# Low parts of weight pages: a negative copy on ScalarE and an accumulating DMA in place of a VectorE subtraction

## The chip, the cores and the metric

One core of one Trainium2 chip. The time is that of one launch of the whole program, in microseconds (us) on the device; lower is better. The runs of the kernel before took 3516.85, 3520.6 and 3525.22 us, median 3520.6.

## What is computed

Two blocks on 1024 tokens of 1024 features, batch 1, all in float32. Cut to what matters here:

```python
# first block, two layers
for l in range(2):
    mod = silu(c) @ w_ada[l] + b_ada[l]                    # shift, scale, gate, twice
    h = rms_norm(x) * (1 + scale_a) + shift_a
    proj = h @ w_in[l]                                      # GLA (4 heads) and MLA (4 heads)
    x = x + gate_a * (concat(gla(proj), mla(proj)) @ w_out[l])
    h = rms_norm(x) * (1 + scale_f) + shift_f
    x = x + gate_f * (square(relu(h @ w_mlp_up[l])) @ w_mlp_down[l])   # 1024 -> 4096 -> 1024
# second block, one layer
z = rms_norm(x) @ w_in                                      # gMLP, RG-LRU and S5 side by side
x = x + mix(z) @ w_out
x = x + moe(rms_norm(x))                                    # 16 experts, two for each token
```

The matmuls are made to float32 accuracy. TensorE takes operands of the type fp32r, so each matrix is held as two: hi, the rounded value, and lo, the rest. A product is three matmuls, hi x hi, hi x lo (lo of the activations) and lo x hi (lo of the weights).

## The kernel before

**Weight pages.** Weights are streamed. A raw page (tag wr, two buffers; in the MLP's up product also e) comes by a load on SP's queue. `split` (L129) makes the two parts: ScalarE copies the raw page to hi (tag wh, L131), and VectorE subtracts, lo = raw - hi (tag wl, L132). There are two buffers of wh and two of wl. A raw page is free for the next load when the subtraction has read it.

```python
    def split(self, src, hi, lo, eng=None):
        self.nc.scalar.activation(hi, src, AF.Copy)
        self.split_ins = (eng or self.nc.vector).tensor_sub(lo, src, hi)
```

Three places make weight pages: `wpage` (L134; `wcols`, L143, calls it), `page` in `mlp` (L1051), and the page of the first quarters in `mlp` (L1090). Activations are split by `split` too (L1229, and the pieces in `put`, L1160 to L1168, and elsewhere), as are the weights of the experts.

**Where pages are used.** The output projection of each layer (L975 to L984) goes through eight pages of 1024 x 128 (512 KB) for the first half of the tokens and the same eight for the second; for each page it loads a piece xo of the residual on POOL's queue (L980), makes 24 matmuls into one PSUM tile (tag ps) and adds the residual on VectorE (L983). `norm_T` makes the operands B11 ... T4 of the MLP in quarters, with sums and differences of quarters.

**The MLP by seven products.** Each pair of 128-column blocks of w_mlp_up, cut into the quarters a11, a12 (upper rows) and a21, a22, goes through `seven` (L1101): POOL (GpSimd) makes s1 = a21 + a22 (L1106), s2 = s1 - a11 (L1107), a21 = a11 - a21 in place (L1108) and s4 = a12 - s2 (L1109). `page` then splits two quarters of 128 x 512 (256 KB) at a time into one wh and one wl buffer, and each quarter is multiplied with one operand by 12 matmuls (hi, hi, lo for each of the four slices). There are 16 pairs in a layer. For the first seven the first quarter's product has been made ahead, so that six products are left ("six-product pairs"); the other nine have all seven. Results get a ReLU on ScalarE, a square on ScalarE or POOL (L1083) and go to DRAM by SP's queue.

The down product runs plain groups of four rows (pages of 512 KB, `plain`, L1206), then *windows*: up to four pairs of hidden features at once, by `seven` again, over four column blocks ("units", 26 in both layers, 14 of them with four pairs), then plain groups again. Within a window `operands` (L1170) makes sums and differences of activations on POOL or VectorE, and `into_x` (L1190) adds results into x, partly on POOL (L1197). In both layers the modulation columns of a later part (w_ada times the condition) are computed beside the MLP ("ada columns"), on VectorE.

**What sets the order.** The program is written as a sequence; a scheduler places each instruction on its engine's list by its own simulated timeline before the program is compiled, with each tile's buffers given out in the order of the code. Each engine then runs its list in order and waits for semaphores. A DMA that POOL issues stands in POOL's list and waits there for its inputs, ahead of what comes after it. SP issues the weight loads, POOL and ACT some others.

Of the kernel before, what the change touches and what calls it, by code (L numbers as in the profile page):

```python
# [15 lines left out]
D = 1024  # L16
# [12 lines left out]
GD = 1  # L29
# [30 lines left out]
class Base:  # L60
    def __init__(self, nc, tc, ctx, I):
# [8 lines left out]
        self.R = ("X", "Y", "Z", "M")   # pages of x, of h's two halves, and of the phase's own  # L70
        self.uid = 0
        self.tab, self.tab_ins = None, []   # the ACT table load in force, and what has used it
# [25 lines left out]
    # ---- small helpers  # L98
# [3 lines left out]
    def mm3(self, out, terms):  # L102
        """terms: list of (wh, wl, xh, xl); out = sum w^T x to float32 accuracy"""
        n = len(terms)
        for i, (wh, wl, xh, xl) in enumerate(terms):
            self.mm(out, wh, xh, start=(i == 0), stop=False)
            self.mm(out, wh, xl, start=False, stop=False)
            self.mm(out, wl, xh, start=False, stop=(i == n - 1))

    def table(self, name):  # L110
        """the ACT table set of what follows, loaded after the last use of the one before"""
        with ExitStack() as st:
            for i in self.tab_ins:
                st.enter_context(self.tc.issue_after(i))
            self.tab = self.nc.scalar.preload_act_table_set(name).ins
        self.tab_ins = []

    def act(self, *a, **k):
        """an activation that needs the table set in force"""
# [9 lines left out]
    def split(self, src, hi, lo, eng=None):  # L129
        """hi + lo == src, both float32r"""  # L130
        self.nc.scalar.activation(hi, src, AF.Copy)  # L131
        self.split_ins = (eng or self.nc.vector).tensor_sub(lo, src, hi)  # L132

    def wpage(self, pieces, a, b, eng=None, tag="wr"):  # L134
        """pieces: list of (index function on the [128,a,b] tile, dram ap)."""
# [4 lines left out]
        self.split(raw, hi, lo)  # L140
        return hi, lo

    def wcols(self, w, c0, n=128):  # L143
        """w dram [K, M]: columns c0..c0+n as [128, K/128, n]"""
# [3 lines left out]
    def rinv(self, psum, n, out, u=None):  # L148
        """out = (psum/n + eps)^-1/2; with a spare tile u, with a Newton step"""
# [21 lines left out]
    def sigmoid_(self, out, x):  # L171
        """out = sigmoid(x) for x >= -40, x in SBUF or PSUM (exp/ln table)"""
# [5 lines left out]
class Block1(Base):  # L178
# [14 lines left out]
    def cols(self):  # L193
        """per-feature vectors on partitions"""
# [17 lines left out]
    # ---- conditioning  # L212
# [7 lines left out]
    def ada_steps(self, l, js, tags=("wr",), kn=2):  # L220
        """mod columns of the vectors js of layer l, onto their biases, kn * 128 rows a step"""
# [27 lines left out]
    # ---- start  # L249
    def start(self):  # L250
        """the first half of x, and the first columns (K half 0, then 1) of the first layer's shift and scale"""
# [25 lines left out]
    def low_load(self, l, kh, i, tag):  # L277
        """columns of m_kpe and g_a with the first of m_q, or the rest of m_q with m_kv: rows of a K half"""
# [5 lines left out]
    def ada_first(self, q):  # L284
        """shift and scale of layer 0: columns of a K half"""
# [20 lines left out]
    def x_done(self, kt, hf, spill, eng=None, tag="t2"):  # L306
        """a tile of x is final: its part of the sum of squares, and its copy in DRAM"""
# [15 lines left out]
    def norm_half(self, hf, s1, sh, kts=range(NT)):  # L323
        """h of a half: rms norm of x times s1 plus sh, as hi and lo"""
# [28 lines left out]
    def adaptive(self, l, j):  # L353
        """scale and shift columns of a norm: vectors j (shift) and j + 1 (scale)"""
# [44 lines left out]
    # ---- hybrid mixer  # L399
    def weave(self, *streams):  # L400
        """streams of (generator, steps a turn), to the end of all"""
# [8 lines left out]
    def mixer(self, l, side=None):  # L410
# [12 lines left out]
        # k_pe and the gate's low rank columns, then m_q, m_kv; the first half of the tokens first  # L423
# [24 lines left out]
        # GLA q and k  # L448
# [23 lines left out]
        def norms(hf):  # L472
            """low rank norms -> hi/lo"""
# [15 lines left out]
        def decays(hf):  # L489
            """GLA gate: cumulative log decay within chunks of 128"""  # L490
# [21 lines left out]
        def pe_units():  # L512
            """rotary parts before their norms: k_pe (on both 64-partition halves) and q_pe of all heads"""
# [35 lines left out]
        def low_first():  # L549
            """the first half of the tokens, as the columns of shift and scale come"""  # L550
# [39 lines left out]
        # ---- GLA values, token-major  # L590
# [23 lines left out]
        # ---- GLA  # L614
# [4 lines left out]
        def gla_in(hf, T):  # L619
            """attention within chunks (keys on partitions), one power of two of the distance at a time"""  # L620
# [5 lines left out]
            # q with the other head's rows at zero  # L626
# [39 lines left out]
        def gla_out(hf, T):  # L666
            """outputs and state, two chunks at a time"""
# [19 lines left out]
            # q decayed from the chunk's start, with the other head's rows at zero  # L687
# [45 lines left out]
        def go_units():  # L733
            """g_o: silu, to DRAM"""
# [14 lines left out]
        # ---- MLA, beside the GLA  # L749
        scale = float(192 ** -0.5)  # L750
        mh, ml = [None] * 8, [None] * 8      # 0..3 GLA, 4..7 MLA
# [17 lines left out]
        def behind(g):  # L769
            """not before the chunks' steps of GD steps ago"""  # L770
# [17 lines left out]
        def mla_steps():  # L788
            # values of all heads, token-major
# [20 lines left out]
            def rope_stack(head):  # L810
                """hi and lo of a head's rotary part, one above the other"""
# [42 lines left out]
            def scores(head, qb):  # L854
                """scores of 128 queries, and their maximum"""
# [23 lines left out]
            def exps(banks, st):  # L879
                """probabilities times their sum, and the sum by banks"""  # L880
# [89 lines left out]
        # ---- output projection and residual, the first half of the tokens first  # L970
# [16 lines left out]
    # ---- MLP  # L987
    def norm_T(self, hf, s1, sh):
        """h of a half, as operands of the products by quarters (K halves by token halves; Strassen's, Winograd's form):
        T1 = B12 - B11, T2 = B22 - T1, T3 = B22 - B12, T4 = B21 - T2"""  # L990
# [47 lines left out]
    def mlp(self, l, following, side=None, early=None, late=()):  # L1038
# [12 lines left out]
        def page(srcs):  # L1051
            n = srcs[0].shape[1]
            hi, lo = self.pg("wh", (128, 2, n, 128), F32R), self.pg("wl", (128, 2, n, 128), F32R)
            for i, s in enumerate(srcs):
                self.split(s, hi[:, i], lo[:, i])
# [11 lines left out]
        def plus(p, t, tag=None):  # L1067
            """p + t, in t or in a tile of its own"""
# [19 lines left out]
        for u in range(NPRE + 1):  # L1088
            if u < NPRE:
# [3 lines left out]
                self.split(raw, hi, lo)  # L1093
# [6 lines left out]
        def seven(K, js, fin, m1=None):  # L1100
            """the four quarters of a product from seven products; with m1, the first quarter is there already"""  # L1101
# [51 lines left out]
        # down: tiles plainly, then windows of four pairs by quarters from the pair J0 to J, then plainly  # L1153
# [108 lines left out]
class Block2(Block1):  # L1262
# [19 lines left out]
    # ---- S5 parameters (depend on weights alone)  # L1282
    def s5_prep(self):
# [15 lines left out]
        def exp_tanh(dst, src, scale, tmp, tmp2):  # L1299
            """dst = exp(2 * scale * src)"""  # L1300
# [11 lines left out]
        # powers of the modulus, n = 0..8  # L1312
# [5 lines left out]
        # phase  # L1318
# [15 lines left out]
        def cmul_steps(dr, di, ar, ai, br, bi, tmp, eng):  # L1334
            """d = a * b (complex), d distinct from a, b"""
# [26 lines left out]
        # (lam_bar - 1) / lam  # L1362
# [14 lines left out]
        # B bar and C^T  # L1377
# [8 lines left out]
        # x -> state, as [(8 tokens, last first; 16 channels), state]  # L1386
# [9 lines left out]
        for th in range(2):  # L1396
# [13 lines left out]
            # state -> y  # L1410
# [17 lines left out]
        # response within 8 tokens, zero padded to the left  # L1428
# [20 lines left out]
        # phases of the states at the starts of 8-token chunks  # L1449
# [26 lines left out]
    # ---- S5 over 128 chunks of 8 tokens  # L1476
    def s5_x(self, w):
        """x by position in the chunk: [128 chunks, group, position (last first), channel]"""
# [24 lines left out]
    def s5(self, xt, th):  # L1503
        """outputs before the gelu: [128 chunks, position, tile, group of the tile, channel]"""
# [41 lines left out]
        # states before each chunk  # L1546
# [27 lines left out]
    def s5_gelu(self, ytm):  # L1574
        """gelu, then channels on partitions"""
# [35 lines left out]
    # ---- RG-LRU parameters  # L1611
    def lru_prep(self):
        """decay rate -8 softplus(-lambda), per channel"""
# [8 lines left out]
        # log1p(exp(-|lam|)) = 2 atanh(z), z = s / (2 - s)  # L1622
# [14 lines left out]
    def mixer2_load(self):  # L1637
        """block diagonal gates; W_s^T, with the later half of keys cut for the earlier half of positions; b_s over the rows of a head"""
# [14 lines left out]
    def lru_gates(self, bx, gt):  # L1653
        """bx becomes the gated input; also the recurrence gates and tanh(log a)"""
# [29 lines left out]
    def lru_scan(self, bx, rt):  # L1684
        """states, in place of tanh(log a)"""
        nc = self.nc
        V, G, ACT = nc.vector, nc.gpsimd, nc.scalar
        for j, (rp, thp) in enumerate(rt):
            prev = 0.0
            for hf in range(2):  # L1690
# [5 lines left out]
                # 1 - a^2 = -tanh(log a) (1 + a^2)  # L1696
# [17 lines left out]
    def sgu(self, vt, hf):  # L1714
        """v becomes W_s v + b_s"""
# [44 lines left out]
    def mixer2(self):  # L1760
# [61 lines left out]
        # ---- output projection, residual  # L1822
# [738 lines left out]
```

## Time and profile before

| | |
|---|---|
| runs | 3516.85, 3520.6, 3525.22 us; median 3520.6 |
| span of the profiled execution | 3517.2 us |
| TensorE matmul (PE) busy | 3190.6 us, 91% |
| VectorE (DVE) busy | 2557.0 us, 73% |
| ScalarE (ACT) busy | 1670.0 us, 47% |
| GpSimd (POOL) busy | 1385.6 us, 39% |
| the two subtraction groups of L132, 331 + 174 instructions | 367.1 + 178.3 us of DVE |

The profile is of one execution, and its span is the time from the first to the last instruction. An engine's busy time counts its own work; issuing a DMA is not counted. Matmuls whose weight load is hidden appear back to back, so PE at 100% in a stretch means that nothing kept it waiting there. A line number with an operation names a group of instructions; "out<-in" are the program's tiles.

### The profile page before, as it was taken

The numbers are of one execution on the slowest core, as the hardware profiler recorded it, in microseconds if no ns is written. First come the engines' busy times: TensorE is split into PE (matmuls) and PEld (weight loads), VectorE is DVE, ScalarE is ACT, GpSimd is POOL, SyncE is SP. The second block draws the span as 40 slices with busy tenths as digits, with TensorE's granted clock in tenths as the row PEclk, the third lists the DMA queues.
The fourth block names the chain that finished last, engine by engine and source line by source line (L and its number), as shares of the span: only waits on it lengthen the run. The fifth ranks groups of instructions, "written<-read, shape, count | busy, mean of one in ns | idle before, by whom it ended". The sixth has DMA issues, their size and how long they took to land. (4 is left out here: it accounts for less than half of the span.)

```text
span 3517.2 us, 42552 instructions
## 1 busy us (share of the span) xinstructions
PE 3190.6 (91%) x14714; PEld 2524.4 (72%) x14714; DVE 2557.0 (73%) x3737; ACT 1670.0 (47%) x2819; POOL 1385.6 (39%) x1176
## 2 busy tenths in 40 slices
PE   5998899899898889999898999997889999699995
PEld 3776678687776677777686788775667766588884
DVE  8778765768879998677756655779985344677867
ACT  4545764532233445556755434323445243466753
POOL 4145411663436763246303654445742313211114
PEclk9999999999999999999999999999999999899998
DMA  6433124346632224121123433522251223589974
GB/s 218 117 96 105 58 64 134 111 150 215 207 129 88 83 91 137 55 67 70 35 77 101 147 116 110 176 78 89 91 162 48 66 75 102 210 279 326 334 269 174
DMA packets 327341, 462.57 MB, mean 132 GB/s; under 512 B 25697, under 2 KB 189825, under 8 KB 327121
## 3 DMA queue, kind: packets, MB, share of 16 engines
q1 hardware_dynamic: 300496, 375.74, 33.2%
q0 software_dynamic: 25472, 83.46, 6.9%
q8 instruction: 117, 1.92, 0.2%
q14 instruction: 104, 0.84, 0.1%
q10 hardware_dynamic: 1152, 0.61, 0.1%
HBM read 383.45 MB, written 77.33 MB: 131 GB/s over the span
## 5 line engine op out<-in xcount | busy, mean ns | idle before, releaser
L131 ACT ACTIVATE wh<-wr 128x1024 fp32r<-128x1024 f32 (+5 forms) x331 | 263.1, 795 | 495.3 <-PE ps L100 314.6
L100 PE MATMUL ps<-Y,wh 128*128 128x512 f32 (+1 forms) x1454 | 475.9, 408 | 17.7 <-ACT wh L131 7.4
L132 DVE TENSOR_TENSOR wl<-wr,wh 128x1024 fp32r<-128x1024 f32 (+5 forms) x331 | 367.1, 1110 | 132.1 <-ACT wh L131 130.3
L100 PE MATMUL ps<-M,wh 128*128 128x512 f32 (+1 forms) x1174 | 382.4, 406 | 9.4 <-ACT wh L131 5.5
L100 PEld LDWEIGHTS ps<-Y,wh 128*128 128x128 f32 (+1 forms) x1454 | 278.4, 194 | 92.0 <-ACT wh L131 11.9
L100 PE MATMUL ps<-Y,wl 128*128 128x512 f32 (+1 forms) x727 | 292.2, 403 | 24.0 <-DVE wl L132 24.0
L100 PE MATMUL ps<-Z,wh 128*128 128x512 f32 (+1 forms) x882 | 281.1, 400 | 3.9 <-ACT Z L342 3.4
L2283 DVE TENSOR_TENSOR X<-Y,X 128x1024 fp32r<-128x1024 f32 x192 | 233.4, 1233 | 58.0 <-ACT X L2279 50.4
L100 PEld LDWEIGHTS ps<-M,wh 128*128 128x128 f32 (+1 forms) x1174 | 223.7, 193 | 66.6 <-ACT wh L131 8.4
L100 PE MATMUL ps<-M,wl 128*128 128x512 f32 (+1 forms) x587 | 237.8, 406 | 20.2 <-DVE wl L132 20.0
L2279 ACT ACTIVATE X<-Y 128x1024 fp32r<-128x1024 f32 x192 | 203.1, 1061 | 96.6 <-PE ps L100 46.9
L100 PEld LDWEIGHTS ps<-Z,wh 128*128 128x128 f32 (+1 forms) x882 | 165.4, 190 | 50.3 <-issue 7.9
L100 PE MATMUL ps<-X,wh 128*128 128x512 f32 (+1 forms) x562 | 181.3, 402 | 2.5 <-ACT wh L131 1.7
L132 DVE TENSOR_TENSOR wl<-a,wh 128x512 fp32r<-128x512 f32 (+3 forms) x174 | 178.3, 1031 | 7.1 <-ACT wh L131 6.6
L100 PEld LDWEIGHTS ps<-Y,wl 128*128 128x128 f32 (+1 forms) x727 | 139.4, 192 | 61.2 <-DVE wl L132 30.7
L100 PE MATMUL ps<-Z,wl 128*128 128x512 f32 (+1 forms) x441 | 174.5, 398 | 5.1 <-DVE wl L132 5.1
L100 PE MATMUL pS<-X,Z 128*128 128x512 f32 x576 | 155.8, 398 | 2.1 <-ACT Z L131 2.1
L100 PE MATMUL ps<-X,Z 128*128 128x512 f32 x576 | 154.4, 395 | 0.8 <-DVE X L2283 0.8
L100 PEld LDWEIGHTS ps<-M,wl 128*128 128x128 f32 (+1 forms) x587 | 112.7, 192 | 54.2 <-DVE wl L132 30.0
L100 PE MATMUL pS<-Y,wh 128*128 128x512 f32 x434 | 140.4, 404 | 5.3 <-ACT wh L131 3.2
L100 PE MATMUL ps<-X,tg 128*128 128x512 f32 x576 | 142.7, 395 | 1.1 <-DVE tg L132 0.6
L1106 POOL TENSOR_TENSOR a<-wr,wr 128x512 f32<-128x512 f32 (+3 forms) x38 | 46.7, 1230 | 229.8 <-DMA wr<-w_mlp_down 84.8
(856 smaller groups left out, 8109.4 us busy)
## 6 DMA issues: line engine op xcount, KB each, us to landing
Y<-expert_w_gate SPq DMA_DIRECT2D x64, 512.0 KB, 6.4
Y<-expert_w_up SPq DMA_DIRECT2D x64, 512.0 KB, 6.4
Y<-expert_w_down SPq DMA_DIRECT2D x64, 512.0 KB, 7.5
wr<-w_mlp_up SPq DMA_DIRECT2D x58, 512.0 KB, 4.1
wr<-w_mlp_down SPq DMA_DIRECT2D x58, 512.0 KB, 3.8
wr<-w_in SPq DMA_DIRECT2D x49, 512.0 KB, 3.8
bt<-w_ada SPq DMA_DIRECT2D x96, 256.0 KB, 3.4
hd<-t SPq DMA_DIRECT2D x70, 256.0 KB, 2.4
```

The costliest lines, as they stand in the source:

```text
L100: self.last_mm = self.nc.tensor.matmul(out, lhsT, rhs, start=start, stop=stop)
L131: self.nc.scalar.activation(hi, src, AF.Copy)
L132: self.split_ins = (eng or self.nc.vector).tensor_sub(lo, src, hi)
L1106: G.tensor_add(s1, a21, a22)
L2279: nc.scalar.activation(hi, raw, AF.Copy)
L2283: (nc.gpsimd if pool else nc.vector).tensor_sub(lo, raw, hi)
```

## The change

A new function `split_w` takes the place of `split` at the three places where weight pages are made outside the experts. Hi is the same copy. ScalarE then writes the negative of the raw page, rounded to fp32r, into the low part's buffer, and a DMA, issued by POOL, adds the raw page to that buffer in SBUF (accum_op add): lo = -hi + raw. VectorE has no part in it. Activations and the experts keep `split`. The rest of the diff takes out comments, which moves the line numbers after it by 7 (L1106 becomes L1113; the new copy is L138, the DMA L139).

```diff
+    def split_w(self, src, hi, lo):
+        nc = self.nc
+        nc.scalar.activation(hi, src, AF.Copy)
+        nc.scalar.activation(lo, src, AF.Copy, scale=-1.0)
+        nc.gpsimd.dma_start(lo, src, accum_op=OP.add)
...
     def wpage(self, pieces, a, b, eng=None, tag="wr"):
...
         hi, lo = self.pg("wh", (128, a, b), F32R), self.pg("wl", (128, a, b), F32R)
-        self.split(raw, hi, lo)
+        self.split_w(raw, hi, lo)
         return hi, lo
...
             for i, s in enumerate(srcs):
-                self.split(s, hi[:, i], lo[:, i])
+                self.split_w(s, hi[:, i], lo[:, i])
...
                 self.last_w = nc.sync.dma_start(raw, wu[:, 256 * u:256 * u + 128].rearrange("(k p) c -> p k c", p=128))
                 hi, lo = self.pg("wh", (128, 8, 128), F32R), self.pg("wl", (128, 8, 128), F32R)
-                self.split(raw, hi, lo)
+                self.split_w(raw, hi, lo)
```

There are 539 such splits: 156 of 128x1024 elements (512 KB), 296 of 128x512 (256 KB), 28 each of 128x128, 128x256 and 128x384, and three of 128x640, together 171 MB. The scheduler makes its lists anew, so other instructions move too.

POOL in the up product, a six-product pair, as its list was before: here s1, s2, the difference in place and s4 of a pair, then the squares of earlier results.

```order
L1106 TENSOR_TENSOR a_1155_5629<-wr_5625,e_5627 128x512
L1107 TENSOR_TENSOR a_1156_5630<-a_1155_5629,wr_5625 128x512
L1108 TENSOR_TENSOR wr_5625<-wr_5625 128x4x128
L1109 TENSOR_TENSOR a_1157_5631<-e_5627,a_1156_5630 128x512
L1083 TENSOR_TENSOR rl_5582<-rl_5582 128x512
L1083 TENSOR_TENSOR t_1142_5545<-t_1142_5545 128x512
L1083 TENSOR_TENSOR t_1147_5579<-t_1147_5579 128x512
```

The four additions stood together. The same place, POOL's list after; wl_6007 is a page of the pair before, wl_6042 is the pair's own page of s2 and s1, wl_6078 that of a21 and s4.

```order
L1113 TENSOR_TENSOR a_1214_6034<-wr_6028,e_6030 128x512
L1114 TENSOR_TENSOR a_1215_6035<-a_1214_6034,wr_6028 128x512
L139 DMA wl_6007<-wr_5913 128x4x128
L1115 TENSOR_TENSOR wr_6028<-wr_6028 128x4x128
L1116 TENSOR_TENSOR a_1216_6036<-e_6030,a_1215_6035 128x512
L1090 TENSOR_TENSOR rl_5984<-rl_5984 128x512
L139 DMA wl_6042<-a_1215_6035 128x512
L139 DMA wl_6042<-a_1214_6034 128x512
L1090 TENSOR_TENSOR t_1200_5945<-t_1200_5945 128x512
L139 DMA wl_6078<-wr_6028 128x4x128
L139 DMA wl_6078<-a_1216_6036 128x512
L1090 TENSOR_TENSOR t_1205_5981<-t_1205_5981 128x512
```

The DMA of s2, the first that the pair's first product needs, now stands behind all four additions and a square, and the DMA of the pair before stands between the second addition and the third.

POOL in a unit of the down windows, before: the additions of a unit between the making of operands (L1181 to L1186, L1168) and the additions into x (L1197, into Z).

```order
L1106 TENSOR_TENSOR a_1857_9118<-wr_9114,wr_9116 128x512
L1181 TENSOR_TENSOR e_9081<-bt_9083,e_9081 128x512
L1197 TENSOR_TENSOR Z_4353<-Z_4353,rl_9042 128x512
L1107 TENSOR_TENSOR a_1858_9119<-a_1857_9118,wr_9114 128x512
L1108 TENSOR_TENSOR wr_9114<-wr_9114 128x4x128
L1183 TENSOR_TENSOR rl_9087<-bt_9083,rl_9087 128x512
L1109 TENSOR_TENSOR a_1859_9120<-wr_9116,a_1858_9119 128x512
L1197 TENSOR_TENSOR Z_4353<-Z_4353,t_1837_9039 128x512
L1186 TENSOR_TENSOR a_1844_9082<-a_1844_9082,rl_9087 128x512
L1168 TENSOR_TENSOR tg_9111<-a_1844_9082,tg_9110 128x512
```

And after: the first DMAs of the unit's pages stand among them.

```order
L1113 TENSOR_TENSOR a_1857_9308<-wr_9304,wr_9306 128x512
L1190 TENSOR_TENSOR rl_9277<-bt_9273,rl_9277 128x512
L139 DMA wl_9316<-wr_9304 128x4x128
L1114 TENSOR_TENSOR a_1858_9309<-a_1857_9308,wr_9304 128x512
L1115 TENSOR_TENSOR wr_9304<-wr_9304 128x4x128
L139 DMA wl_9354<-wr_9306 128x4x128
L1193 TENSOR_TENSOR a_1844_9272<-a_1844_9272,rl_9277 128x512
L1204 TENSOR_TENSOR Z_4376<-Z_4376,t_1837_9228 128x512
L139 DMA wl_9354<-a_1857_9308 128x512
L1116 TENSOR_TENSOR a_1859_9310<-wr_9306,a_1858_9309 128x512
L139 DMA wl_9316<-a_1858_9309 128x512
```

The DMA of s2 (a_1858) is the last of these rows: it comes behind s4 and behind the DMAs of a12 (wr_9306) and s1 (a_1857), which the second page holds.

## Rows read from the trace of the kernel before

**Rows 1.** The page's first part: busy time, share of the span, instructions.
```profile
PE 3190.6 (91%) x14714; PEld 2524.4 (72%) x14714; DVE 2557.0 (73%) x3737; ACT 1670.0 (47%) x2819; POOL 1385.6 (39%) x1176
```

**Rows 2.** The page's costliest groups: busy us, mean ns | idle before, and its releaser.
```profile
L131 ACT ACTIVATE wh<-wr 128x1024 fp32r<-128x1024 f32 (+5 forms) x331 | 263.1, 795 | 495.3 <-PE ps L100 314.6
...
L132 DVE TENSOR_TENSOR wl<-wr,wh 128x1024 fp32r<-128x1024 f32 (+5 forms) x331 | 367.1, 1110 | 132.1 <-ACT wh L131 130.3
...
L132 DVE TENSOR_TENSOR wl<-a,wh 128x512 fp32r<-128x512 f32 (+3 forms) x174 | 178.3, 1031 | 7.1 <-ACT wh L131 6.6
```

**Rows 3.** Waits of PE, by releaser: us, count, longest.
```profile
PE ps L100 <- DVE wl L132: 59.8, 43, 9.4
...
PE pS L100 <- DVE wl L132: 36.2, 15, 3.7
```

**Rows 4.** Groups of VectorE by form: one subtraction whose source is in PSUM.
```profile
L132 DVE TENSOR_TENSOR Z<-pO,Z 128x512 fp32r<-128x512 f32 x48 | 33.0, 687 | 48.2 <-ACT Z L131 48.2
```

**Rows 5.** Stretches: us, busy (xcount) of PE, PEld, DVE, ACT, POOL; PEclk, DMA, GB/s.
```profile
612.00:671.00 59.00, 44.95 (x175) 34.56 (x174) 40.99 (x41) 33.42 (x54) 30.39 (x17) 0.88 0.30 94
763.00:1000.00 237.00, 218.73 (x930) 176.03 (x929) 200.92 (x256) 79.98 (x134) 94.81 (x68) 0.93 0.67 212
1048.00:1326.00 278.00, 238.72 (x953) 184.84 (x951) 269.95 (x272) 114.70 (x204) 197.18 (x125) 0.94 0.27 86
2052.00:2225.00 173.00, 173.00 (x765) 143.26 (x764) 89.58 (x129) 72.00 (x121) 79.53 (x61) 1.00 0.40 132
2310.00:2576.00 266.00, 229.64 (x951) 176.24 (x949) 248.64 (x403) 94.81 (x172) 155.66 (x123) 0.97 0.27 86
```

**Rows 6.** DMA issues: KB each, median us from issue to landing.
```profile
rl<-xd POOLq DMA_DIRECT2D x32, 256.0 KB, 3.2
...
X<-s5m POOLq DMA_DIRECT2D x2, 512.0 KB, 4.6
...
xd<-Z POOLq DMA_DIRECT2D x16, 256.0 KB, 2.3
...
wr<-w_mlp_up SPq DMA_DIRECT2D x58, 512.0 KB, 4.1
```

**Rows 7.** Line L980, DMA issues on POOL: ns shortest/mean/longest, first and last start.
```profile
L980 POOL DMA_DIRECT2D rl<-xd x16: 536/543/572, 1702.0 to 1886.4; - x16
```

**Rows 8.** Timeline, output projection: start, us, instruction [idle before <- releaser].
```profile
545.04 1.06 ACT L131 ACTIVATE wh<-wr 128x1024 fp32r<-128x1024 f32 x1 [4.75 <-PE ps L100]
...
550.48 1.06 ACT L131 ACTIVATE wh<-wr 128x1024 fp32r<-128x1024 f32 x1 [3.84 <-PE ps L100]
...
556.36 0.39 PE L100 MATMUL ps<-X,wl 128*128 128x512 f32 x1
```

**Rows 9.** Timeline, a six-product pair of the up product.
```profile
700.12 0.63 ACT L131 ACTIVATE wh<-wr 128x512 fp32r<-128x512 f32 x1 [1.10 <-PE ps L100]
...
707.23 1.29 POOL L1106 TENSOR_TENSOR a<-wr,wr 128x512 f32<-128x512 f32 x1 [4.00 <-DMA wr<-w_mlp_up]
...
713.72 0.63 ACT L131 ACTIVATE wh<-wr 128x512 fp32r<-128x512 f32 x1 [1.10 <-PE ps L100]
```

**Rows 10.** Timeline, units of a down window.
```profile
1145.18 0.63 ACT L131 ACTIVATE wh<-wr 128x512 fp32r<-128x512 f32 x1 [4.78 <-DVE rl L1070]
...
1151.87 1.74 POOL L1107 TENSOR_TENSOR a<-a,wr 128x512 f32<-128x512 f32 x1
...
1159.29 0.50 PE L100 MATMUL ps<-M,wl 128*128 128x512 f32 x1 [1.05 <-DVE wl L132]
...
1193.81 0.63 ACT L131 ACTIVATE wh<-wr 128x512 fp32r<-128x512 f32 x1 [4.81 <-DVE rl L1070]
```

## The prediction

> **What bounds the kernel now.** I read the page's first part, then TensorE's waits, then busy times by stretch, then timelines of the three places where a weight page is made and used. TensorE is busy for 3190.6 of 3517.2 us, VectorE 2557.0, GpSimd 1385.6 [rows 1]: where no weight is late the kernel runs at the pace of the matmuls, as in 2052:2225, where PE has no gap and the granted clock is 1.00 [rows 5]. The largest waits of PE are for a low part: 59.8 + 36.2 us behind DVE's wl subtraction [rows 3]. They lie in the stretches where DVE is near 97% busy, 1048:1326 (PE idle 39 us), or works beside many transfers, 763:1000 (idle 18 us); 2310:2576 loses 36 us [rows 5]. These are the only places where less VectorE work could give anything: 39 + 36 + 18 = 93 us at the very most.
>
> **What is removed.** 539 subtractions (the order of both kernels shows all of them gone from DVE). 505 of them took 367.1 + 178.3 us [rows 2]. The same subtraction on 512 columns takes 687 ns when its source is in PSUM [rows 4], and about 1.03 to 1.1 us on average here [rows 2], since DVE and POOL, both reading SBUF, hold each other up. On the path only the 93 us above can come back.
>
> **What is added.** (1) On ACT 539 more copies, as long as the hi copies: 263.1 us for 331 of them [rows 2], 0.62 us each for most of the other 208, so some 390 us on an engine that is 47% busy. (2) On POOL 539 DMA issues of 0.54 us [rows 7], 290 us, which stand in POOL's order and wait there for ACT's negative copy; what is behind them waits too. (3) A transfer between ACT's copy and PE's use. No row shows an accumulating DMA. Below: a plain store out of SBUF from POOL's queue, 256 KB, 2.3 us from issue to landing; nearest: a plain load on that queue, 3.2 us for 256 KB, 4.6 for 512 KB [rows 6]. An accumulating transfer must also read what it adds to; if every byte counts twice, the upper ends are 6.4 and 9.2. For 256 KB I take 4.0, between the row for its bytes (3.2) and the row for twice as many (4.6); for 512 KB 6.0, the 4.6 plus one more step of 1.4 (what 256 KB more cost in these rows). Lower ends 2.3 and 3.3 (the store's row, one third less than the load's, applied to 512 KB). Transfers grow by 171 MB (156 pages of 512 KB, 296 of 256 KB, 87 smaller), read once or twice: where it is 0.67 (763:1000) that is not free, elsewhere it is hidden.
>
> The transfer is an add in the DMA engines, and the Trainium skill (Collectives: The Full Stack, section The bandwidth ceiling) says that such an add needs two source reads and so doubles the read traffic; with the fit of its page DMA: Bandwidth & Descriptors (Anatomy of one DMA, SWDGE path: 2.0 us plus bytes at 436 GB/s) an estimate would be 3.2 us for 256 KB and 4.4 for 512 KB. The plain loads of [rows 6] are already at 3.2 and 4.6, so the trace does not carry the fit's small slope for a doubled read. By these two figures the sum below would come to 3800 us.
>
> **Where the new latency lands.** Four loops; each was closed with time to spare, or just closed, before.
>
> Pages of 512 KB used for one half of the tokens. ACT's hi copy starts when the page before last is done: 545.04 and 550.48, 5.44 us apart; the first wl matmul comes 5.88 us after the hi copy's start (556.36) [rows 8]. Now hi 1.06 + negative 1.06 + 0.1 + 6.0 = 8.2 us. With two buffers a page ends 5.0 us after its low part, so two periods are 8.2 + 5.0 and one is 6.6: 1.17 us more. There are 32 such pages in the two output projections and 16 in the last down groups (56 us), and some 39 with a similar gap in the starts of the MLPs and in the second block, at 0.9 (34 us). In 612:671 and its twin (PE idle 14 of 59 us [rows 5]) no other page stands between release and use; there the 14 pages pay about 1.4 us more each, 20. Sum 110.
>
> MLP up, six products (7 pairs in each layer). The raw weights were free for the next load as soon as DVE's subtraction had read them; now they are held until the DMA lands. Before, the period is 713.72 - 700.12 = 13.6 us, PE bound [rows 9]. The loop now, from the release of the page of a21 and s4: copies and a POOL multiplication in front 2.0, landing 4.0, load 0.4 + 4.1 [rows 6], then POOL in its new order: four adds of 1.3 (L1106's is 1.29 [rows 9]), one issue 0.55, one multiplication 1.3, all ahead of the next pair's first wl DMA, landing 4.0, less 0.45 for the two hi matmuls that go first: 21.1. With PE's 13.6 that makes two periods: (21.1 + 13.6) / 2 = 17.35, 3.75 more. 14 x 3.75 = 53. Before, s2 had only to be added second and subtracted by DVE: this is the place where a queue is passed, not only a latency added.
>
> MLP up, seven products (9 pairs in each layer). Here the same loop takes one period: 2.0 + 4.0 + 4.5 + 6.5 + 4.0 - 0.45 + 5.44 = 26.0. Before: 19.2 in the second layer (173 us for 9 [rows 5]), about 25 in the first, where DVE has the ada columns beside it (237 us for 9.5 [rows 5]). 9 x 6.8 + 9 x 1.0 = 70.
>
> MLP down, windows. 26 units, 14 of them with four pairs; a full one takes (1193.81 - 1145.18) / 2 = 24.3 us, and PE waits 1.05 us for the low part of s2, which POOL started at 1151.87 [rows 10]. The loop now, from the release that lets a22 be split: two copies 1.4, landing 4.0, load 4.0; POOL, in order: seven tensor operations at 1.5 (1.29 alone, 1.74 beside DVE: [rows 9, 10]) and four issues, 12.7, until s2's DMA is issued; the rest of its landing 3.5; PE to the end of the next page 7.7. That is 33.3, 9.0 more. 14 x 9.0 = 126; the 12 smaller units, with smaller transfers, at 6.0 make 72. Sum 198.
>
> Not on the path: pages that are made long ahead of their use, as beside the GLA and in the second block's first products; ACT's extra copies (47% busy); the experts, which keep their split.
>
> **Sum.** 110 + 53 + 70 + 198 = 431 us. DVE's relief is in the 1.5 of POOL and in the first layer's 1.0. The profiled span is 3517.2, the runs' median 3520.6, so 3.4 is added for what lies around: 3952, given as 3950. With 6.4 and 9.2 the same four loops give 286 + 86 + 157 + 313 = 842, so 4360; with 2.3 and 3.3 they give 14 + 29 + 9 + 114 = 166, so 3690.
>
> **Rivals.** (A) The forecast, 3950, loops closed by a landing near 4 and 6 us: 0.61. (B) The landing is short, as for a plain store, and only POOL's order costs: 3690, chance 0.17; for it speaks that nothing touches HBM, against it that each byte is read twice. (C) The adding itself is slow (8 us for 256 KB, 14 for 512 KB or more): pages 515 + 100, pairs 111 + 216, windows 398, together 1340, so 4860; chance 0.12. No row speaks against it, since none shows the operation. (D) On the other side: the 93 us come back and nothing else is lost, 3430. The place is 1048:1326, where POOL and DVE hold each other up (1.74 us for a POOL add of 1.29 alone); it decides if the low part lands within 2 us of the negative copy, no later than DVE's 1.1 us and its queue. Even the store's 2.3 us is above that: 0.06. (E) Relief and loss cancel, 3520: 0.04. That the change does not do what it says is out: the order shows the 539 subtractions gone and 539 DMAs in their place.
>
> **Chances.** A measurement of this kernel can tell about 0.2% from no change. Slower by more than that: A, B and C, 0.90; within it: E, 0.04; faster: D, 0.06. The range reaches from 3660 (B with a little relief) to 4370 (A at its upper ends); C, D and E stay outside, which is about 2 in 10 with the tails.
>
> **What would show it.** The DMA rows wl<-wr and wl<-a give the landing times: 4.0 and 6.0 as median. DVE's busy time falls by 500 to 600 us, ACT's rises by 390. PE's waits of wl move from DVE to the DMA and grow to several hundred us; output-projection pages start 6.6 us apart instead of 5.44, six-product pairs 17 us, window units 33 us. POOL's first up add waits for a later load. A granted clock below the 0.88 to 0.97 of the stretches that already wait [rows 5] would add to A. The forecast is wrong if the wl DMAs land in under 2.5 or over 7 us, or if POOL's order lets s2's DMA go without the adds in front.

## The result and the profile after

The changed kernel took 4148.5 us (4137.0 to 4152.6), the one before 3519.7 (3516.9 to 3525.2): a ratio of 1.178, 95% interval 1.176 to 1.180. The forecast was slower, 3950 us with a range of 3660 to 4370: the time lies in it, but the loss of 629 us is half as large again as the 431 of the sum.

The first part of the page after, to be held against [rows 1]:

```profile
span 4147.0 us, 43929 instructions
...
PE 3393.6 (82%) x14714; PEld 2609.4 (63%) x14714; DVE 2178.0 (53%) x3198; ACT 1990.1 (48%) x3358; POOL 1828.0 (44%) x1715
```

The span grew by 629.8. PE does the same 14714 matmuls, but is busy 203 us longer, and stands still 427 us longer (3517.2 - 3190.6 = 327 before, 4147.0 - 3393.6 = 753 after). DVE gave up 379 us of work. GpSimd's busy time, unlike the other engines', does count its DMA issues: the records of the 539 new ones cover 631 us, partly at the same time as those of its other work. The waits of PE in the kernel after (total us, times, longest), against [rows 3]:

```profile
PE ps L100 <- DMA wl<-wr: 340.8, 145, 7.8
PE pS L100 <- ACT wh L137: 75.5, 28, 6.0
PE ps L100 <- DMA wl<-e: 48.4, 22, 6.2
PE ps L100 <- ACT wh L137: 43.2, 37, 4.0
PE pS L100 <- DMA wl<-a: 25.9, 15, 2.9
```

DVE no longer stands in this list for a low part; the DMA that took its place does, with 340.8 + 48.4 + 25.9 = 415 us where DVE had 59.8 + 36.2. Where the 629.8 us lie, by stage (each begins with the first load of its weights in the trace, the experts with their first gather; us):

| stage | before | after | more |
|---|---|---|---|
| start, mixer of layer 0 | 507.0 | 527.4 | 20.4 |
| output projection, layers 0 and 1 | 92.8, 118.8 | 121.2, 145.0 | 28.4, 26.2 |
| MLP up, layers 0 and 1 | 376.2, 328.4 | 500.3, 471.5 | 124.1, 143.1 |
| MLP down, layers 0 and 1 | 383.3, 394.3 | 541.0, 509.1 | 157.7, 114.8 |
| mixer of layer 1 | 409.5 | 408.9 | -0.6 |
| second block: mixer, output projection | 208.6, 203.0 | 215.0, 216.5 | 6.4, 13.5 |
| experts (split unchanged) | 495.3 | 491.1 | -4.2 |

Six sevenths are in the two MLPs. A stretch that has the same matmuls in both kernels shows how: eight seven-product pairs of layer 1, first before, then after (columns as in [rows 5]).

```profile
2048.00:2200.00 152.00, 152.00 (x673) 125.84 (x672) 77.22 (x111) 58.86 (x102) 74.04 (x56) 1.00 0.34 110
```

```profile
2458.00:2683.00 225.00, 176.12 (x674) 133.92 (x673) 37.94 (x57) 88.45 (x160) 127.73 (x112) 0.92 0.73 140
```

DVE's work halves (77 to 38 us), and it was never what PE waited for here. PE, which had no gap, now has 49 us of gaps, and the same matmuls take 24 us more at a granted clock of 0.92 where it was 1.00. So a third of this stretch's loss stands in slower matmuls and two thirds in gaps. That is an account of where the time lies; it does not show that the slower matmuls cost time of their own, since a loop that a landing closes can hide them. A timeline of PE in the output projection of the kernel after shows what a wait can leave behind (start, us, instruction, idle before):

```profile
648.26 0.62 PE L100 MATMUL ps<-X,wl 128*128 128x512 f32 x1 [2.41 <-DMA wl<-wr]
648.68 1.05 PE L100 MATMUL ps<-X,wh 128*128 128x512 f32 x2
649.54 0.63 PE L100 MATMUL ps<-X,wl 128*128 128x512 f32 x1
...
652.01 0.39 PE L100 MATMUL ps<-X,wl 128*128 128x512 f32 x1
```

After 2.41 us without work the matmuls start at 0.62 us each, and return to 0.39 in less than four microseconds; their starts go from 0.43 to 0.23 us apart, the two levels 1.2 and 2.4 GHz. The granted clock is 0.54 from 648.2 to 651.9 us and 1.00 in the microsecond after. The wait of 1.75 us that ended at 640.11 was not followed by such a fall: 1.00 from 640 to 646.

### The profile page after: what moved, and what is told of

Its sections match the earlier page's. It is cut to its first block, busy times and chain, and to the rows that moved or that the text cites. A ratio compares the mean times of both kernels' runs of the same rounds, so it can differ in the third digit from the quotient of the medians.

```text
span 4147.0 us, 43929 instructions
## 1 busy us (share of the span) xinstructions
PE 3393.6 (82%) x14714; PEld 2609.4 (63%) x14714; DVE 2178.0 (53%) x3198; ACT 1990.1 (48%) x3358; POOL 1828.0 (44%) x1715
## 5 line engine op out<-in xcount | busy, mean ns | idle before, releaser
L139 POOL DMA_DIRECT2D wl<-wr x331 | 393.2, 1190 | 741.0 <-ACT wl L138 653.7
L100 PE MATMUL ps<-Y,wh 128*128 128x512 f32 (+1 forms) x1454 | 504.5, 431 | 21.2 <-ACT wh L137 14.5
L100 PE MATMUL ps<-M,wh 128*128 128x512 f32 (+1 forms) x1174 | 411.1, 434 | 9.2 <-ACT wh L137 7.5
L100 PE MATMUL ps<-M,wl 128*128 128x512 f32 (+1 forms) x587 | 260.8, 445 | 130.6 <-DMA wl<-wr 110.7
L100 PE MATMUL ps<-Z,wh 128*128 128x512 f32 (+1 forms) x882 | 292.2, 413 | 13.5 <-ACT wh L137 9.4
L100 PEld LDWEIGHTS ps<-M,wh 128*128 128x128 f32 (+1 forms) x1174 | 245.2, 212 | 74.7 <-ACT wh L137 14.0
L1077 DVE TENSOR_TENSOR t<-ps,bt 128x512 f32<-128x512 f32 x58 | 40.1, 691 | 436.4 <-PE ps L100 389.8
L138 ACT ACTIVATE wl<-wr 128x1024 fp32r<-128x1024 f32 (+5 forms) x331 | 259.7, 785 | 13.9 <-PE ps L100 12.8
L139 POOL DMA_DIRECT2D wl<-a x174 | 260.7, 1543 | 10.2 <-ACT wl L138 9.1
L1077 DVE TENSOR_TENSOR t<-ps,t 128x512 f32<-128x512 f32 x116 | 79.9, 689 | 256.9 <-PE ps L100 256.8
L100 PE MATMUL ps<-X,wl 128*128 128x512 f32 (+1 forms) x281 | 119.9, 427 | 48.7 <-DMA wl<-wr 46.8
```

The lines of the kernel that those rows point to most:

```text
L100: self.last_mm = self.nc.tensor.matmul(out, lhsT, rhs, start=start, stop=stop)
L138: nc.scalar.activation(lo, src, AF.Copy, scale=-1.0)
L139: nc.gpsimd.dma_start(lo, src, accum_op=OP.add)
L1077: V.tensor_add(o, p, t)
```

## Experiments

**Where the cost is: the copy, the DMA, or its adding.** Three kernels take the change apart. In the first VectorE adds, where the DMA did:

```diff
-        nc.gpsimd.dma_start(lo, src, accum_op=OP.add)
+        nc.vector.tensor_add(lo, lo, src)
```

> As the changed kernel, with ScalarE's negative copy, but VectorE adds the raw page to it in place of the accumulating DMA. It tells the DMA's part from that of ScalarE's 539 extra copies. If the DMA (its landing and its place in GpSimd's order) is what costs, the time is near that of before plus the copy's 0.6 to 1.06 us where a page's loop closes: 3560 us, 3510 to 3620. If ScalarE's extra copies are a large part of the 629 us, it is over 3700.

3559.9 us, beside 3527.1 for the kernel before on the same chip (one run of each). ScalarE's copies, which the sum had at nothing, cost about 33 us; the rest, nearly 600, is the DMA's.

In the second the DMA copies and does not add:

```diff
-        nc.gpsimd.dma_start(lo, src, accum_op=OP.add)
+        nc.gpsimd.dma_start(lo, src.bitcast(F32R))
```

> The same DMAs, issued at the same places by GpSimd, but copying the raw page over the low part without adding (the low part is then the raw page: the subtraction is left out). If it is the adding that makes the landing long (4.9 us for 512 KB, 5.3 for 256 KB) and the issue 0.87 to 1.4 us, landings fall to 2.3 to 3.3 us, the issue to 0.54, and the time to 3700 us (3650 to 3800). If any transfer at this place costs as much, it stays at 4100 or more.

4052.0 us: neither of the two. Part of it is not the copy's: with the raw page as low part tokens go to other experts, the matmuls grow to 14946, and the experts take 661 us where they took 491. Up to the experts' first gather it is 3389.0 us, against 3655.9 with the adding and 3021.9 before. The page's rows on transfers of this kernel (KB each, median us to landing), and behind them those of the kernels with only whole pages and only quarters by the adding DMA, described below:

```profile
wl<-wr POOLq DMA_DIRECT2D x154, 512.0 KB, 3.1
wl<-a POOLq DMA_DIRECT2D x138, 256.0 KB, 3.0
wl<-wr POOLq DMA_DIRECT2D x126, 256.0 KB, 3.4
```

```profile
wl<-wr POOLq DMA_DIRECT2D x154, 512.0 KB, 4.9
```

```profile
wl<-a POOLq DMA_DIRECT2D x138, 256.0 KB, 5.3
wl<-wr POOLq DMA_DIRECT2D x124, 256.0 KB, 5.4
```

Adding makes the landing, counted from the issue's start, 4.9 us where a copy needs 3.1, and 5.3 where it needs 3.0. The records of the issue on GpSimd are longer, too: in the changed kernel these are the rows of the line (ns shortest/median/longest), against the 0.54 of [rows 7], which the copies of 2048 bytes a partition also take (0.56):

```profile
L139 POOL DMA_DIRECT2D wl<-wr x331: 837/943/2506, 70.8 to 3606.3; - x166
L139 POOL DMA_DIRECT2D wl<-a x174: 845/1422/2545, 725.9 to 3167.3; - x174
```

But such a record runs on beside the next instruction. Where GpSimd goes on without a gap, the next one starts 0.60 us (median) after the issue of a whole page, 0.58 after that of an a tile and 0.80 after that of a raw quarter; with plain copies it is 0.57, 0.58 and 0.79. So the adding hardly holds up GpSimd's list; the landing is what it makes longer.

And the queue's row (packets, MB, share of 16 DMA engines) for the changed kernel, then for the one that copies: the same bytes, with half as much again of the engines' time.

```profile
q0 software_dynamic: 169136, 254.87, 32.8%
```

```profile
q0 software_dynamic: 169424, 255.92, 21.6%
```

In the third the copy is issued by ScalarE, behind its own negative copy, so that it no longer stands in GpSimd's order:

```diff
-        nc.gpsimd.dma_start(lo, src, accum_op=OP.add)
+        nc.scalar.dma_start(lo.bitcast(F32), src)
```

> The plain copy of the raw page over the low part (nothing is added: the subtraction is left out), issued by ScalarE right behind its negative copy, so that it stands in no order of GpSimd's. The data sends the experts into more blocks, so the time up to the first gather of the experts is compared: 3022 us before, 3656 in the changed kernel, 3389 with the copy issued by GpSimd. If GpSimd's order and issue are a cause of their own beside the landing, it falls to 3220 (3150 to 3290). If the landing alone counts, it stays over 3350.

3256.9 us at the first gather (3919.9 in all), within the bounds. Its copies land about as soon as those that GpSimd issued:

```profile
wl<-wr ACTq DMA_DIRECT2D x154, 512.0 KB, 3.0
wl<-a ACTq DMA_DIRECT2D x138, 256.0 KB, 2.7
```

So what went is GpSimd's order and issue (the transfers go by another queue as well, but land no later). The kernels make a ladder of the 634 us that are lost up to that point:

| step | first gather, us | more |
|---|---|---|
| before | 3021.9 | |
| negative copy on ScalarE, VectorE adds | 3062.1 | 40 |
| a transfer takes VectorE's place (ScalarE's queue, no adding) | 3256.9 | 195 |
| it is issued by GpSimd | 3389.0 | 132 |
| it adds | 3655.9 | 267 |

The steps are differences of whole kernels with lists of their own, so a few tens of us could change places.

**Which pages.** Two kernels use `split_w` for a part of the pages only and `split` for the rest, first for the pages that are split whole:

```diff
             for i, s in enumerate(srcs):
-                self.split_w(s, hi[:, i], lo[:, i])
+                self.split(s, hi[:, i], lo[:, i])
```

> The accumulating DMA only for pages that are split whole (output projections, first quarters, plain down groups, the mixers); the quarters of the seven products are split with VectorE's subtraction. In the changed kernel the pairs' periods (20 and 28 to 33 us against 13.4 and 19 to 25) and the down units' (34.5 against 24.3) hold about 450 of the 629 us, so about 180 are left here: 3700 us, 3650 to 3760. If queueing of all the DMAs on one another and on GpSimd is the cause, the whole pages alone cost much less: under 3610.

3661.7 us, 135 more than the 3527.1 beside it. The counterpart changes `wpage`, and the page of the first quarters likewise, back and leaves the quarters:

```diff
         hi, lo = self.pg("wh", (128, a, b), F32R), self.pg("wl", (128, a, b), F32R)
-        self.split_w(raw, hi, lo)
+        self.split(raw, hi, lo)
         return hi, lo
```

> The counterpart: the accumulating DMA only for the quarters of the seven products (346 of the 539 splits), whole pages with VectorE's subtraction. If the loops are independent, it is 3520 + 629 - what the whole pages alone cost: near 3970 us (3900 to 4030), and the two parts add up to 629 within 40. If the two share a queue or the clock, the parts add up to clearly less or more than 629.

4013.0 us, 486 more than the 3527.1. Together 620 of 629: the two parts hardly touch each other. The third narrows it to pages of which the prediction had most as "made long ahead", those of the mixers and of the second block:

```diff
-                wh, wl = self.wcols(I["w_out"][l], 128 * ct)
+                wh, wl = self.wcols(I["w_out"][l], 128 * ct, sp=self.split)
...
-        self.split_w(raw, hi, lo)
+        (sp or self.split_w)(raw, hi, lo)
```

with the MLP's three places on `split` as well.

> The accumulating DMA only for weight pages of the mixers and of the second block's projections; output projections of the first block and the whole MLP are split with VectorE's subtraction. In the changed kernel these stages lost some 40 us of the 629: 3555 us, 3535 to 3580. If the pages made ahead of their use cost nothing and VectorE's relief pays, it is 3515 or less.

3576.6 us, 1.4% slower (interval 1.2 to 1.5%). Most of these 50 us are not in the sum: by the stages of the table the profiled run lost 20, 8 and 15 us in the three mixers, which the sum had at nothing, and 11 in the second block's output projection, of which it had a part. No stage got more than 4 us shorter by VectorE's relief.

**GpSimd's order in the MLP.** The four sums and differences of `seven` go to VectorE, which has room now; the DMAs stay where they are:

```diff
-            G.tensor_add(s1, a21, a22)
-            G.tensor_sub(s2, s1, a11)
-            G.tensor_sub(a21, a11, a21)
-            G.tensor_sub(s4, a12, s2)
+            V.tensor_add(s1, a21, a22)
+            V.tensor_sub(s2, s1, a11)
+            V.tensor_sub(a21, a11, a21)
+            V.tensor_sub(s4, a12, s2)
```

> The changed kernel with the four sums and differences of the seven products on VectorE (53% busy) where GpSimd made them, so that the DMA issues of a pair no longer stand behind them in GpSimd's list. If GpSimd's order is the second cause beside the landing, six-product pairs fall from 20 to 17 us, seven-product pairs from 28 to 33 to about 25, full down units from 34.5 to 29: 3890 us, 3820 to 3980. If only the landing counts: over 4080.

3979.9 us, 169 less than the changed kernel, at the upper end of what was expected. The periods fell in every loop (below). So the additions ahead of a DMA in GpSimd's list are a cause beside the landing, as the prediction had it, but the smaller one. The run does not tell their place in the list from their own time on GpSimd, nor from the end of VectorE's long subtractions in the down windows (last section).

**The low part needed later.** TensorE takes all matmuls with the high part first:

```diff
             self.mm(out, wh, xl, start=False, stop=False)
-            self.mm(out, wl, xh, start=False, stop=(i == n - 1))
+        for i, (wh, wl, xh, xl) in enumerate(terms):
+            self.mm(out, wl, xh, start=False, stop=(i == n - 1))
```

and likewise in `prod`.

> The changed kernel with another order of the matmuls of a page: all products with the high part first, then those with the low part. TensorE then has 16 matmuls of 0.23 us (3.7 us) to do on a whole page, and 8 (1.8 us) on a quarter, before it needs the DMA, where it had two. If the landing at the first use is what costs, whole pages (135 us when alone) come back nearly all and quarters 1.4 us for each landing in their loop, about 70 us: 3950 us, 3880 to 4030. If GpSimd's order alone holds the pages up, little changes: over 4090.

4143.6 us: nothing gained, and the theory that the landing costs only at the first use falls. Its waits of PE show where the time went:

```profile
PE ps L100 <- DMA wl<-wr: 218.1, 101, 13.9
PE ps L100 <- ACT wh L138: 131.4, 61, 10.2
```

The wait for the low part is 123 us shorter, and that for the next high part 88 longer than above. In the output projection ScalarE's timeline names the reason: the high copy of a page waits for its load (start, us, instruction, idle before and what ended it).

```profile
565.38 1.06 ACT L138 ACTIVATE wh<-wr 128x1024 fp32r<-128x1024 f32 x1 [5.54 <-DMA wr<-w_out]
...
572.94 1.06 ACT L138 ACTIVATE wh<-wr 128x1024 fp32r<-128x1024 f32 x1 [5.03 <-DMA wr<-w_out]
...
580.19 1.06 ACT L138 ACTIVATE wh<-wr 128x1024 fp32r<-128x1024 f32 x1 [4.73 <-DMA wr<-w_out]
...
587.54 1.06 ACT L138 ACTIVATE wh<-wr 128x1024 fp32r<-128x1024 f32 x1 [4.83 <-DMA wr<-w_out]
```

The load waits in turn for the DMA that still reads the raw buffer; SP's queue in this stage (520 to 634 us):

```profile
SPq L146 <- DMA wl<-wr: 102.3, 14, 14.8
```

Before, the raw buffer came free with VectorE's subtraction (1.06 us for the high copy [rows 8] and 1.1 for the subtraction [rows 2], so about 2.2 after the copy began); now it is held until the landing. To test that, the two output projections got a third raw buffer (the page e), with the high part first as well:

```diff
-                wh, wl = self.wcols(I["w_out"][l], 128 * ct)
+                wh, wl = self.wpage([(None, I["w_out"][l][:, 128 * ct:128 * ct + 128].rearrange("(k p) c -> p k c", p=128))], 8, 128,
+                                    tag=("wr", "wr", "e")[(8 * hf + ct) % 3])
```

> The changed kernel with the high part first (4144 us, no gain) and, in the two output projections alone, a third raw buffer (the page e). There ScalarE's high copies waited for w_out's loads, and these for the accumulating DMA that still read the raw buffer: landing 7.3 us, load 5, two copies 2.3, 14.6 us for two pages. If this loop of the raw buffers is what bounds the pages once the low part's use is put off, the two stages (114 and 141 us) fall to about 96 and 122: 4105 us in all, 4085 to 4120. If GpSimd's order (the residual's load ahead of the DMA) bounds them, they stay within 5 us and the time is over 4130.

```profile
566.16 1.06 ACT L138 ACTIVATE wh<-wr 128x1024 fp32r<-128x1024 f32 x1 [2.09 <-PE ps L100]
...
571.79 1.06 ACT L138 ACTIVATE wh<-wr 128x1024 fp32r<-128x1024 f32 x1 [2.15 <-DMA wr<-w_out]
...
578.53 1.06 ACT L138 ACTIVATE wh<-e 128x1024 fp32r<-128x1024 f32 x1 [2.77 <-DMA e<-w_out]
...
583.96 1.06 ACT L138 ACTIVATE wh<-wr 128x1024 fp32r<-128x1024 f32 x1 [2.34 <-DMA wr<-w_out]
```

The pages are now 5.9 us apart where they were 7.4, so the raw buffer does close the loop there. By the measure of the table above the two stages fell from 123 and 141 us to 98 and 129. The whole time was 4138.5 us all the same, above the bounds: the other stages together are 35 us longer than with the high part first alone. (With one more buffer the next stage's first load also comes earlier, so a part of this only moves the boundary.) The MLP, whose loops are as long as before, is what the next gain would have to come from. A third raw buffer there was not tried.

**Both, and the order alone.** High part first with the additions on VectorE (the two diffs above together):

> Both in the changed kernel: high part first, and the sums and differences on VectorE. If the two causes are separate, the gains add up: about 3720 us (3650 to 3800), with the rest being landings in the pairs' and units' loops. If both act on the same wait, it is no better than the better of the two by more than 40 us.

3959.3 us, 21 less than the additions alone: the second case. The same order of matmuls in the kernel before, whose VectorE subtracts:

> The kernel before (VectorE subtracts), with the same order of matmuls: high part first. TensorE waited 59.8 + 36.2 us for low parts. If these waits are latency at the first use, up to 96 us come back: 3460 us, 3430 to 3500. If they are VectorE's throughput in its full stretches, the wait only moves to the end of the page: 3510 to 3530.

3521.0 us against 3527.0, a ratio of 0.998 (interval 0.997 to 0.999). It is the only kernel here that beats both, by 6 us: the second case, not the 60 us of the first. Its largest waits of PE show that the wait moved, from the low part to VectorE's later work and to ScalarE's next high part:

```profile
PE pS L100 <- DVE rl L1072: 29.5, 3, 16.3
PE pS L100 <- ACT wh L132: 23.2, 21, 2.7
PE ps L100 <- DVE wl L133: 19.9, 16, 4.1
```

## Why the prediction was right, and where its sum was off

Periods from the trace (from one first addition of `seven` to the next; us), with the prediction's:

| loop | before | predicted | after | additions on VectorE | copy, ScalarE's queue |
|---|---|---|---|---|---|
| six-product pair, layers 0 / 1 | 12.9 / 12.9 | 17.35 | 19.3 / 19.8 | 17.0 / 17.1 | 15.2 / 14.7 |
| seven-product pair, layers 0 / 1 | 24.1 / 19.0 | 26.0 | 32.6 / 28.1 | 28.7 / 23.1 | 26.6 / 21.2 |
| full down unit, layer 0 | 24.4 | 33.3 | 34.9 | 30.6 | 28.4 |

- **What bounds, and the sign.** Right. PE waited for low parts more, not less, and VectorE's relief gave nothing back: in the stretch of layer 1's pairs it halved DVE's work and PE lost 49 us. Rival D is out; so are C, whose landings (8 and 14 us) were not seen, and E. B's short landing is what the copying kernel has: there GpSimd's order and 3 us of landing cost 367 us up to the first gather, twice the 170 that B was given (some 40 of the 367 are ScalarE's copies). DVE's busy time fell by 379 us where 500 to 600 were forecast (last section), and ACT's rose by 320 where 390 were.
- **The landing** was the term that mattered most, and it was mis-sized in both directions. The changed kernel's own trace gives no landing times; those of the kernels with only whole pages and only quarters do: for 512 KB 6.0 was taken and 4.9 measured, for 256 KB 4.0 and 5.3. What failed is the size taken from single plain loads. In the trace with only quarters, a quarter that was issued when the DMA before it in GpSimd's list had landed took 4.3 us (median of 89), and one issued while that DMA was still under way took 5.6 (205 of them); for whole pages it is 4.6 and 5.5. So 4.0 was near for a quarter by itself, the 2.0 put on top of it for a page was far too much (4.3 to 4.6), and a term was missing: the two quarters of a page go out one behind the other. That is read from the traces; no run issued the quarters singly.
- **The issue on GpSimd**, taken from plain loads at 0.54 us [rows 7], was right or nearly so: 0.6 to 0.8 until the next instruction starts (above).
- **The pairs.** The loops were the right ones. With 5.4 in place of 4.0 alone, the six-product loop is 2.0 + 5.4 + 4.5 + 5.2 + 0.55 + 1.3 + 5.4 - 0.45 = 23.9, and (23.9 + 13.6) / 2 = 18.8, where 19.3 and 19.8 were measured. (The 13.6 before was read from one interval [rows 9]; the mean is 12.9, which alone is worth 14 x 0.7 = 10 us.) The seven-product loop is 2.0 + 5.4 + 4.5 + 6.5 + 5.4 - 0.45 + 5.44 = 28.8, measured 28.1 in layer 1. In layer 0 it is 32.6: there the DMA engines, which also carry the ada columns' loads, are 0.91 busy, and the landings in the kernel with only quarters are 6.4 us, with which the loop comes to 30.8; the rest is open. So the pairs cost 14 x 6.6 + 9 x 8.5 + 9 x 9.1 = 251 us instead of 123. This is two thirds of what the sum missed.
- **The windows** came out at 34.9 against 33.3, from their first unit to their last 133 + 80 = 213 us more against 198. The formula holds with measured terms: the landing is 5.2 there (kernel with only quarters), and in one unit GpSimd's list took 11.6 us, from the first addition (1299.44) to the start of s2's issue (1311.06, last section), where 12.7 was put. So 1.4 + 5.2 + 4.0 + 11.6 + 5.2 + 7.7 = 35.1.
- **Pages of 512 KB.** Put at 110. Whole pages alone cost 135, but 50 of these lie in the mixers and the second block, which leaves 85 for the output projections and the MLPs. The sum is near by luck: the two output projections lost 28.4 + 26.2 = 55 us where 37 was put (32 pages at 1.17), and the MLPs' pages less than was put. In the projections the loop named (the low part's buffers) was not the only one: the raw buffer, held until the landing, closes a second one of about the same length, which the prediction had seen for the pairs and not here.
- **What was costed at nothing.** ScalarE's copies cost 33 to 40 us, though the engine is 47% busy. The pages made long ahead cost most of the 50, not 0.
- **The clock** was named as something that would add, and left out of the sum. PE is busy 203 us longer with the same matmuls. In the windows the granted clock is 0.83, where it was 0.94 [rows 5]:

```profile
1215.00:1545.00 330.00, 215.40 (x777) 162.33 (x777) 213.37 (x148) 125.95 (x234) 218.83 (x173) 0.83 0.60 113
```

The loops above come out near their measured periods without a term for it, so whether the lower clock added time is open. That the gaps of PE alone, 427 us more, are close to the sum's 431 is a coincidence: the terms of the sum missed one by one.
- **The adding.** The prediction set a rule of the Trainium skill beside the rows (Collectives: The Full Stack, The bandwidth ceiling: such an add doubles the read traffic). The packets' times agree with it: one of 2048 bytes took 187 ns at the median where the copy's took 101, one of 512 bytes 71 where it took 42. The reads themselves are not counted in the trace, whose bytes are the same for both. The estimate from the fit in the Trainium skill (DMA: Bandwidth & Descriptors, Anatomy of one DMA), 4.4 and 3.2 us, is not borne out: 4.9 and 5.3, or 4.6 and 4.3 for a transfer with none under way before it.

## What to carry to other kernels

A transfer in place of an engine's work brings a latency into every loop that the work closed: not only that of the consumer, also that of the source's buffer, which stays held until the landing. Count both loops, the issuing engine's list as a third, and the transfer ahead on the same queue, before counting the relief; here the relief of an engine that TensorE hardly waited for brought nothing back. Take an issue's cost in that list from the start of the next instruction, not from the length of its record. And where TensorE begins to wait, look at the granted clock before reading longer matmuls as work: here 203 us of busy time came with 427 us of gaps.

## What the runs showed of the hardware that was not expected

GpSimd can hold VectorE up for far longer than one instruction. In the down windows of the kernel after, a subtraction on 512 columns from SBUF takes 8.44 us, in eight of the units of layer 0 and four of layer 1, while GpSimd goes from one operation to the next without a gap. VectorE and then GpSimd from 1303 us (start, us, instruction):

```profile
1303.22 8.44 DVE L1175 TENSOR_TENSOR X<-bt,X 128x512 fp32r<-128x512 f32 x1
```

```profile
1303.51 1.76 POOL L1114 TENSOR_TENSOR a<-a,wr 128x512 f32<-128x512 f32 x1
1304.77 1.73 POOL L1115 TENSOR_TENSOR wr<-wr 128x512 f32<-128x512 f32 x1
1305.97 1.78 POOL L139 DMA_DIRECT2D wl<-wr  x1
1306.79 2.26 POOL L1193 TENSOR_TENSOR a<-a,rl 128x512 f32<-128x512 f32 x1
1308.02 2.24 POOL L1204 TENSOR_TENSOR Z<-Z,t 128x512 f32<-128x512 f32 x1
1309.22 1.90 POOL L139 DMA_DIRECT2D wl<-a  x1
1309.83 2.94 POOL L1116 TENSOR_TENSOR a<-wr,a 128x512 f32<-128x512 f32 x1
1311.06 2.54 POOL L139 DMA_DIRECT2D wl<-a  x1
```

The group's mean in the changed kernel is 6436 ns, and 1503 in the kernel whose copies ScalarE issues:

```profile
L1175 DVE TENSOR_TENSOR X<-bt,X 128x512 fp32r<-128x512 f32 x12 | 77.2, 6436 | 0.0
```

```profile
L1175 DVE TENSOR_TENSOR X<-bt,X 128x512 fp32r<-128x512 f32 x12 | 18.0, 1503 | 0.0
```

This is about half of why DVE's busy time fell by 379 us and not by the 577 of the subtractions that went: L1175 alone took 100 us more. That it is the chain of GpSimd's operations that keeps VectorE out, and not one of them, is read from the two timelines. The kernel with the four additions on VectorE supports it: with them out of the chain the same group takes 0.68 us at the median (ns shortest/median/longest).

```profile
L1175 DVE TENSOR_TENSOR X<-bt,X x12: 677/678/1123, 1115.6 to 1475.0; 128x512 fp32r<-128x512 f32 x12
```

VectorE's own order is another there, too, so the chain is not the only thing that changed. What the long subtractions cost is not shown: in layer 0's full units (1267 to 1583 us) PE waits for the DMA (69.5 us) and for ScalarE's high copy (38.4 us), never for VectorE.
